# The opening of a two-layer transformer kernel: first value products from un-normed operands, in an order written out by hand

## The chip, the cores and the metric

The kernel runs on one core of one Trainium2 chip. The metric is the device time of one execution in microseconds. Lower is better. The engines are called by the names the profile uses: PE is TensorE (matrix products, 128 x 128), PEld its weight loads, DVE is VectorE, ACT is ScalarE, POOL is GpSimd, and SP is SyncE, which here issues most of the loads from memory (DMA). Each engine runs its own instructions in the order of its program, and waits on semaphores for the others. PE writes its results into eight PSUM banks of 128 x 512 f32, from which ACT or DVE has to fetch them; POOL cannot read them.

## The reference: what is computed

512 latent tokens and 256 context tokens of 1024 features go through two layers. In each layer every token is normed and modulated, goes through attention, and then through a gated feed-forward network. Only the first step of the first layer matters here:

```python
def rms_norm(x):                      # gain left out
    return x * rsqrt(mean(x * x, axis=-1) + EPS)

def modulate(x, shift, scale):
    return rms_norm(x) * (1 + scale) + shift

# layer 0: six vectors of 1024 from the conditioning, for latents (c) and for context (c_ctx)
sh_a, sc_a, g_a, sh_f, sc_f, g_f = split(silu(c) @ mod_w[0] + mod_b[0], 6)
a_lat, a_ctx = modulate(x, sh_a, sc_a), modulate(ctx, csh_a, csc_a)
p = a @ even_w_in                     # 1024 -> 1952; its last 512 columns are the values v
```

The norm factor of a token is one number for the whole token, and stands to the left of the product with the weights: `(r * x * (1 + scale) + shift) @ w` is `r * ((x * (1 + scale)) @ w) + shift @ w`.

## The kernel before

Activations lie with features on the partitions: `X[k]` is the k-th of eight tiles of 128 features by 768 tokens (columns 0 to 511 latents, `LATS`; 512 to 767 context, `CTXS`). Every f32 product is made of three products of the fast f32r kind: each operand is split into a high part (a cast) and a low part (the rest), and high x high, high x low and low x high are summed in PSUM (`three`, lines 780 to 783; `mm3`, lines 319 to 327).

The opening is lines 774 to 932. `mods_pe` (lines 180 to 204) makes the scale (component 1) and shift (component 0) vectors of layer 0. One vector comes in four chunks of 256 features, and a chunk takes four loads of 256 KB, eight products of 32 rows each (line 192), a copy out of PSUM by ACT (line 194), small products with `pick` that bring the chunk onto partitions (line 196), and two additions on DVE (line 200). `mods_pe` is a generator, and `next(scales)` or `next(shifts)` writes one chunk into the program.

The latent columns of all eight X tiles are loaded first and normed (`rms`, line 775): ACT squares each tile, DVE sums the squares, PE adds them over the partitions (line 370), ACT and DVE make the reciprocal root, PE spreads it over all partitions (line 454), and ACT copies it to `r` (line 379). Then, for each k, `scaled` (lines 789 to 795) multiplies X[k] by scale and by r on DVE, ACT casts the high part into `A[k][0]`, and DVE subtracts to get the low part `A[k][1]`. `start_products` (line 785) multiplies token tile t of A[k] by the weights of the values, `w_start[k]` (128 x 512, split on ACT and DVE by `split`), and sums over k into the bank `ov[t]`. There are six token tiles, so six of the eight banks are held for the whole opening. The other two (`PM`, lines 872 to 874) serve all that passes through. The shift reaches the values as a product `shift @ w_start` (line 915), which is copied, split, and added to each of the six banks by two more products (line 926). `put_vs` (lines 857 to 859) copies the six banks to the value tiles `VN` in 24 pieces of 128 x 128, on DVE and ACT in turn.

`A[k]` with two shift columns behind it (`shifted_columns`, lines 797 to 804) is then the operand of the first projections (`project_shifted`, lines 817 to 831, whose products are lines 325 to 327). They need all eight A[k], a free bank, and a weight tile (`load_w`: a load of 512 KB into the buffer `wr`, a cast on ACT, a subtraction on DVE). Beside the projections DVE and POOL compute further modulation vectors as dot products with `cond`, which `load_cond` (lines 162 to 164) loads and passes through Silu behind the opening.

What sets the order: instructions are written in program order, and a planner places each on its engine by a model of the time, so later instructions can move ahead on an engine while an earlier one waits. Where the code says `with in_order(...)` (lines 652 and 653) the instructions written inside it keep their written order on the engines named; others may still be placed between them. In the kernel before, nothing of the opening is written inside such a block. Buffers come in rings by tag (line 37): for example 12 of tag `st`, 3 of `wr`, 3 each of `wh` and `wl`, 8 of `p`, 24 of `b`. A load into a ring waits until an older tile of it has been read for the last time.

Of the kernel before, what the change touches and what calls it, by code (L numbers as in the profile page):

```python
# [15 lines left out]
ON_PE, ON_DVE, ON_ACT = mybir.EngineType.PE, mybir.EngineType.DVE, mybir.EngineType.Activation  # L16
P = 128
D = 1024
# [83 lines left out]
def hybrid_kernel(ctx: ExitStack, tc, I, out):  # L102
# [77 lines left out]
    def mods_pe(l, comp, get, both=None):  # L180

        one = float(comp in (1, 4))
        for v in range(2):
            MOD[l, comp, v] = T(f"mod{l}{comp}{v}", [P, 8]) if both is None else both[:, :, v]
        for c in range(4):
            o = get()
            for k in range(KT):
                if k % 2 == 0:
                    w = T("st" if l == 0 and comp < 2 else ("ph", "pl")[k // 2 % 2], [P, 512])
                    dma(w, I["mod_wp"][PE_MODS.index((l, comp)), c, k // 2])  # L190
                g = slice(32 * (k % 4), 32 * (k % 4) + 32)
                PE.matmul(o[g, :NX], cond_col[:, k], w[:, NX * (k % 2) : NX * (k % 2) + NX], start=k < 4, stop=k > 3)
            t, d = T("p", [P, NX]), get()
            S.copy(t, o[:, :NX])
            for m in range(2):
                PE.matmul(d[:, 2 * m : 2 * m + 2], t[:, m * P : (m + 1) * P], pick, start=True, stop=True)
            for v in range(2):
                r = MOD[l, comp, v][:, 2 * c : 2 * c + 2]
                at = l * 48 + comp * 8 + 2 * c
                V.scalar_tensor_tensor(r, d[:, :4].rearrange("p (m x) -> p m x", x=2)[:, :, v], one,  # L200
                                       modb[:, at : at + 2], op0=ALU.add, op1=ALU.add)
                for m in range(2):
                    MOD[l, comp, v, 2 * c + m] = r[:, m : m + 1]
            yield
# [569 lines left out]
    r = B(tag="nb")  # L774
    rms(X, LATS, r, lambda: PS("t"))
# [9 lines left out]
    def start_products(k, w, tiles):  # L785
        for t in tiles:
            three(ov[t], [x[:, t * P : (t + 1) * P] for x in A[k]], w, k == 0, k == KT - 1)

    def scaled(k, v, c):

        t = B(tag="p")
        h, lo = A[k]
        V.scalar_tensor_tensor(t[:, c], X[k][:, c], MOD[0, 1, v, k], r[:, c], op0=ALU.mult, op1=ALU.mult)
        S.copy(h[:, c], t[:, c])
        V.tensor_tensor(lo[:, c], t[:, c], f(h[:, c]), op=ALU.subtract)
# [61 lines left out]
    def put_vs(vs, kt, o):  # L857
        for p in range(4):
            copy(vs[p][:, kt * P : (kt + 1) * P], o[:, p * P : (p + 1) * P])

# [17 lines left out]
    def load_pair(c):  # L878

        h, lo = (T(x, [P, 2, 512], F32R) for x in ("wh", "wl"))  # L880
        for i in range(2):
            raw = T(("ph", "pl")[i], [P, 512])
            dma(raw, I["w_start"][2 * c + i])
            raws.append(raw)
            ws.append(split(raw, dst=(h[:, i], lo[:, i])))

    def products(c, v):

        for k in (2 * c, 2 * c + 1):
            scaled(k, v, (LATS, CTXS)[v])  # L890
            start_products(k, ws[k], ((0, 1, 2, 3), (4, 5))[v])

    scales, shifts = mods_pe(0, 1, PM), mods_pe(0, 0, PM, shift)
    next(scales)
    load_pair(0)
    next(scales)
# [34 lines left out]
    for t in range(6):  # L931
        put_vs(VN, t, ov[t])
# [1046 lines left out]
```

## Time and profile before

| what | value |
|---|---|
| median of 3 runs | 1563.28 us (1561.6 to 1563.68) |
| span of the profiled execution | 1559.6 us |
| its own time beside the span | the profile gives none beyond the span; the runs lie 2.0 to 4.1 us above it |
| instructions | 26600 |
| PE busy | 1521.7 us, 98% of the span |
| DVE, ACT, POOL busy | 1172.4 (75%), 805.4 (52%), 281.4 us (18%) |
| mean granted PE clock | 0.996 |
| first value product on PE | 23.02 us |
| first product of the first projection | 76.86 us |

The span is the time from the first to the last instruction of one profiled execution. A row of the timeline gives start, length, engine, line, operation, what is written and read, and, in brackets, the idle time before it and what ended that. "x16" means that sixteen instructions were merged into the row. Products are pipelined, so the length of one (0.39 us) is more than the distance to the next (0.23 us). An f32 product that is not split shows as two instructions.

### The profile page before, as it was taken

The numbers are of one execution on the slowest core, as the hardware profiler recorded it, in microseconds if no ns is written. First come the engines' busy times: TensorE is split into PE (matmuls) and PEld (weight loads), VectorE is DVE, ScalarE is ACT, GpSimd is POOL, SyncE is SP. The second block draws the span as 40 slices with busy tenths as digits, with TensorE's granted clock in tenths as the row PEclk, the third lists the DMA queues.
The fourth block names the chain that finished last, engine by engine and source line by source line (L and its number), as shares of the span: only waits on it lengthen the run. The fifth ranks groups of instructions, "written<-read, shape, count | busy, mean of one in ns | idle before, by whom it ended". The sixth has DMA issues, their size and how long they took to land.

```text
span 1559.6 us, 26600 instructions
## 1 busy us (share of the span) xinstructions
PE 1521.7 (98%) x9942; PEld 1355.6 (87%) x9942; DVE 1172.4 (75%) x2348; ACT 805.4 (52%) x1639; POOL 281.4 (18%) x317
## 2 busy tenths in 40 slices
PE   6999989999999999999999999999999999999998
PEld 4687867887998999998999999877789999899997
DVE  4495887576698497896878777888877778678686
ACT  5355588776474243242423345557767445454453
POOL 0173634333000010111111110381002000000000
PEclk9999999999999999999999999999999999999999
DMA  9458263104453554756666655140015223324232
GB/s 327 146 165 260 65 166 91 24 7 162 137 201 96 172 192 155 241 162 219 195 231 235 232 200 193 43 146 2 1 53 165 60 94 125 98 92 129 83 101 88
DMA packets 82129, 216.63 MB, mean 139 GB/s; under 512 B 10832, under 2 KB 18896, under 8 KB 82000
## 3 DMA queue, kind: packets, MB, share of 16 engines
q1 hardware_dynamic: 66640, 163.02, 32.8%
q0 software_dynamic: 13056, 48.77, 9.2%
q10 hardware_dynamic: 2304, 3.15, 0.5%
q8 instruction: 78, 1.28, 0.4%
q14 instruction: 51, 0.42, 0.1%
HBM read 187.10 MB, written 23.07 MB: 135 GB/s over the span
## 4 chain that ended last, share of the span: by engine, by line
PE 88%; DVE 6%; DMA 4%; issue 1%; ACT 1%; SPq 0%; DVEq 0%; ACTq 0%
PE pso L537 5%; PE pss L1416 4%; PE psd L325 4%; PE pss L325 4%; PE pss L1415 4%; PE pss L1414 4%; PE pss L326 4%; PE psd L326 4%; PE pss L327 4%; PE psd L327 4%; PE psd L1416 3%; PE psd L1415 3%; PE psd L1414 3%; PE pst L1414 3%; PE pst L1416 3%; PE pst L1415 3%
## 5 line engine op out<-in xcount | busy, mean ns | idle before, releaser
L312 ACT CAST wh<-wr 128x512 fp32r<-128x512 f32 (+2 forms) x139 | 106.0, 777 | 196.7 <-PE pss L326 37.5
L313 DVE TENSOR_TENSOR wl<-wr,wh 128x512 fp32r<-128x512 f32 (+2 forms) x136 | 126.5, 936 | 69.9 <-ACT wh L312 69.1
L543 ACT ACTIVATE p<-p,sm 128x512 f32<-128x512 f32 (+3 forms) x144 | 104.9, 729 | 29.9 <-DVE sm L547 29.2
L1415 PE MATMUL pss<-b,wh 128*128 128x384 f32 (+1 forms) x302 | 93.5, 310 | 0.0
L1414 PE MATMUL pss<-b,wh 128*128 128x384 f32 (+1 forms) x302 | 93.2, 309 | 0.0
L1416 PE MATMUL pss<-b,wl 128*128 128x384 f32 (+1 forms) x302 | 92.8, 310 | 0.1
L326 PE MATMUL psd<-b,wh 128*128 128x512 f32 (+3 forms) x253 | 86.2, 341 | 0.0
L537 PE MATMUL pso<-ph,b 128*64 128x256 f32 (+1 forms) x400 | 77.0, 351 | 1.0 <-DVE ph L475 0.8
L537 PE MATMUL pso<-pl,b 128*64 128x256 f32 (+1 forms) x400 | 77.0, 351 | 0.1
L325 PE MATMUL psd<-b,wh 128*128 128x512 f32 (+3 forms) x213 | 75.8, 357 | 0.2 <-DVE b L475 0.2
L327 PE MATMUL psd<-b,wl 128*128 128x512 f32 (+3 forms) x213 | 74.5, 351 | 0.0
L326 PE MATMUL pss<-b,wh 128*128 128x256 f32 (+3 forms) x223 | 72.8, 327 | 0.0
L769 PE MATMUL pss<-st,st 128*128 128x512 f32 (+2 forms) x264 | 68.6, 375 | 3.7 <-DVE sm L547 3.4
L325 PE MATMUL pss<-st,wh 128*128 128x512 f32 (+2 forms) x212 | 71.9, 339 | 0.0
L327 PE MATMUL pss<-st,wl 128*128 128x512 f32 (+2 forms) x212 | 71.8, 339 | 0.0
L1416 PE MATMUL psd<-b,wl 128*128 128x384 f32 (+1 forms) x226 | 70.8, 313 | 0.4 <-DVE wl L1402 0.4
L1415 PE MATMUL psd<-b,wh 128*128 128x384 f32 (+1 forms) x226 | 70.7, 313 | 0.0
L1414 PE MATMUL psd<-b,wh 128*128 128x384 f32 (+1 forms) x226 | 70.5, 312 | 0.0
L1401 ACT CAST wh<-ph 128x512 fp32r<-128x512 f32 x80 | 46.4, 620 | 40.1 <-DVE ph L1436 14.4
L1401 ACT CAST wh<-wr 128x1024 fp32r<-128x1024 f32 x40 | 42.1, 1053 | 39.2 <-PE pss L326 10.1
L1401 ACT CAST wh<-pl 128x512 fp32r<-128x512 f32 x80 | 45.9, 619 | 30.6 <-PE pst L1415 9.7
L484 PE MATMUL pst<-ident_r,p 128*128 128x128 f32 x346 | 58.0, 276 | 2.0 <-ACT p L543 0.9
(655 smaller groups left out, 5328.7 us busy)
## 6 DMA issues: line engine op xcount, KB each, us to landing
wr<-in_w_gu_dram SPq DMA_DIRECT2D x88, 512.0 KB, 4.0
wr<-in_w_out_dram SPq DMA_DIRECT2D x32, 512.0 KB, 3.5
wr<-in_w_dn_dram SPq DMA_DIRECT2D x64, 256.0 KB, 2.8
p<-home SPq DMA_DIRECT2D x40, 384.0 KB, 4.7
home<-p POOLq DMA_DIRECT2D x40, 384.0 KB, 5.1
nb<-in_mod_w_dram POOLq DMA_DIRECT2D x48, 256.0 KB, 3.8
rope<-in_mod_w_dram POOLq DMA_DIRECT2D x24, 512.0 KB, 4.3
wr<-in_w_in_dram SPq DMA_DIRECT2D x21, 512.0 KB, 4.8
```

Source lines behind the costliest of these rows:

```text
L312: S.copy(h, r)
L313: (G if eng else V).tensor_tensor(lo, r, f(h), op=ALU.subtract)
L325: PE.matmul(o, wh[:, k], mh[:, c], start=first and k == 0, stop=False)
L326: PE.matmul(o, wh[:, k], ml[:, c], start=False, stop=False)
L327: PE.matmul(o, wl[:, k], mh[:, c], start=False, stop=last and k == n - 1)
L537: ins = PE.matmul(o[64 * i : 64 * i + 64, c], v(kt), t, start=n == 0, stop=n == len(moving[i]) - 1)
L543: S.activation(p[:, c], p[:, c], AF.Exp, bias=nm, scale=-1.0, accum_out=dn)
L769: PE.matmul(o, x, k, start=i == 0, stop=i == 1)
L1401: S.copy(h, t)
L1414: PE.matmul(o, wh, xh, start=first and k == 0, stop=False, skip_group_check=not first)
L1415: PE.matmul(o, wh, xl, start=False, stop=False, skip_group_check=not first)
L1416: PE.matmul(o, wl, xh, start=False, stop=k == 3, skip_group_check=not first)
```

## The change

The opening is written anew. The main parts are these.

- The values are multiplied from un-normed operands. `unnormed(k)` casts X[k] times scale (ACT) and subtracts (DVE); `start_products` uses these, and the norm factor is applied when the banks are fetched (`put_values`), as a factor per token. The operands of the later projections are still normed: `normed_upper` and `normed_lower` make them behind the spread of the norm, the low part for odd k on POOL.
- `with in_order(ON_PE, ON_ACT, ON_DVE)` fixes the order of the opening on three engines. The modulation products stand between the value products, each chunk in two steps: up to ACT's copy, and from the `pick` products on.
- The first scale chunk is computed in two halves of 128 features, and its weights are laid out for that in memory.
- X[k] is loaded whole, in the order of use, together with w_start[k]. The first shift chunk goes into the three `wr` buffers and one of `st`.
- Products of zeros (`keep_running`) run on PE at the start, 9, 2 and 4 of them.
- The bias `shift @ w_start` is no longer added to the banks by products. Two products for each of the two rows spread it, ACT copies it into `cond`, and `put_values` adds it, on DVE for the latent tiles, on POOL for the context tiles.

```diff
     X = [B() for _ in range(KT)]
-    for k in range(KT):
-        dma(X[k][:, LATS], I["xc"][k, :, LATS])
     modb = const("modb", [P, 96])
-    ident_r = const("ident", [P, P], F32R)
+    ident_r = T("ident_r", [P, P], F32R)
...
+    def mod_weights(l, comp, c, tags=None):
+        ws = []
+        tags = tags or (("st",) * 4 if l == 0 and comp < 2 else ("ph", "pl") * 2)
+        for k in range(0, KT, 2):
+            ws.append(T(tags[k // 2], [P, 512]))
+            dma(ws[-1], I["mod_wp"][PE_MODS.index((l, comp)), c, k // 2])
+        return ws
...
+            ws = fetched.get(c) or mod_weights(l, comp, c)
+            single = (l, comp, c) == (0, 1, 0)
+            for part in range(2 if single else 1):
+                n = 1 if single else 2
+                o = get()
+                for k in range(KT):
+                    w = ws[2 * part + k // 4][:, P * (k % 4) :] if single else ws[k // 2][:, NX * (k % 2) :]
+                    g = slice(32 * (k % 4), 32 * (k % 4) + 32)
+                    PE.matmul(o[g, : n * P], cond_col[:, k], w[:, : n * P], start=k < 4, stop=k > 3)
+                t = T("p", [P, NX])
+                S.copy(t[:, : n * P], o[:, : n * P])
+                if halves:
+                    yield
+                d = get()
...
-    r = B(tag="nb")
-    rms(X, LATS, r, lambda: PS("t"))
+    r, rcol = B(tag="nb"), T("rcol", [P, NT // P])
...
+    def start_products(k, tiles):
+        for t in tiles:
+            three(ov[t], [x[:, t * P : (t + 1) * P] for x in U[k]], ws[k], k == 0, k == KT - 1)
+    def unnormed(k):
+        h, lo = U[k] = A[k] if k < 6 else [B(F32R, "p") for _ in range(2)]
+        for v, c in enumerate((LATS, CTXS)):
+            S.activation(h[:, c], X[k][:, c], AF.Copy, scale=MOD[0, 1, v, k])
+            V.scalar_tensor_tensor(lo[:, c], X[k][:, c], MOD[0, 1, v, k], f(h[:, c]), op0=ALU.mult, op1=ALU.subtract)
+    def normed_upper(k):
+        t = normed[k] = B(tag="p")
+        for v, c in enumerate((LATS, CTXS)):
+            V.scalar_tensor_tensor(t[:, c], X[k][:, c], MOD[0, 1, v, k], r[:, c], op0=ALU.mult, op1=ALU.mult)
+        S.copy(A[k][0][:, :NT], t)
+    def normed_lower(k):
+        (G if k % 2 else V).tensor_tensor(A[k][1][:, :NT], normed[k], f(A[k][0][:, :NT]), op=ALU.subtract)
...
+    def start_norm():
+        d = PM()
+        for i in range(NT // P):
+            PE.matmul(d[:, i : i + 1], sums[0][:, i * P : (i + 1) * P], ones[:, :1], start=True, stop=True)
+        S.activation(rcol, d[:, : NT // P], AF.Sqrt, bias=eps, scale=1.0 / D)
+        V.reciprocal(rcol, rcol)
+    def start_spread():
+        for i in range(0, NT // P, 4):
+            n = min(4, NT // P - i)
+            d = PM()
+            spread(d, [rcol[:, x : x + 1].to_broadcast([P, P]) for x in range(i, i + n)])
+            S.copy(r[:, i * P : (i + n) * P], d[:, : n * P])
+    def start_bias():
+        bias = PM()
+        for k in range(KT):
+            PE.matmul(bias[32 * (k % 4) : 32 * (k % 4) + 32], shift[:, k], raws[k], start=k < 4, stop=k > 3)
+        raw = cond[:, :, :NX]
+        S.copy(raw, bias.rearrange("p (v c) -> p v c", v=2))
+        part = [T(x, [P, 512], F32R) for x in ("wh", "wl")]
+        hi, lo = (x.rearrange("p (v c) -> p v c", v=2) for x in part)
+        S.copy(hi, raw)
+        V.tensor_tensor(lo, raw, f(hi), op=ALU.subtract)
+        return part
+    def spread_bias(part):
+        for v in range(2):
+            o = PM()
+            for i, x in enumerate(part):
+                PE.matmul(o, pick_r[:, v : v + 1].to_broadcast([P, P]), x, start=i == 0, stop=i == 1)
+            S.copy(cond[:, v, 512:], o)
+    def put_values(tiles):
+        for t in tiles:
+            for p in range(4):
+                c, at = slice(p * P, (p + 1) * P), slice(t * P, (t + 1) * P)
+                row = cond[:, t // 4, 512 + p * P : 640 + p * P]
+                if t < 4:
+                    V.scalar_tensor_tensor(VN[p][:, at], ov[t][:, c], rcol[:, t : t + 1], row, op0=ALU.mult, op1=ALU.add)
+                else:
+                    S.activation(VN[p][:, at], ov[t][:, c], AF.Copy, scale=rcol[:, t : t + 1])
+                    G.tensor_tensor(VN[p][:, at], VN[p][:, at], row, op=ALU.add)
...
+    early = fetched_w[1, 0] = [T("st", [P, 512]) for _ in range(4)]
+    for m in range(2):
+        for i in (2 * m, 2 * m + 1):
+            dma(early[i], I["mod_wp"][0, 0, i])
+        fetch_x(m)
+    ident_raw = cond[:, 0, :P]
+    dma(ident_raw, I["ident"])
+    for c, ks in ((1, (2, 3)), (2, (4, 5)), (3, (6, 7))):
+        fetched_w[1, c] = mod_weights(0, 1, c)
+        for k in ks:
+            fetch_x(k)
+    fetched_w[0, 0] = mod_weights(0, 0, 0, ("wr", "wr", "wr", "st"))
...
+    def keep_running(n):
+        for _ in range(n):
+            PE.matmul(ov[0], idle[:, :P], idle, start=True, stop=True)
+    with in_order(ON_PE, ON_ACT, ON_DVE):
+        keep_running(9)
+        next(scales)
+        keep_running(2)
+        next(scales)
+        split_start(0)
+        unnormed(0)
+        keep_running(4)
+        start_products(0, (0, 1))
+        next(scales)
+        start_products(0, (2,))
+        next(scales)
+        split_start(1)
+        unnormed(1)
...
+        split_start(7)
+        start_products(4, (3, 4, 5))
+        start_products(5, (0, 1))
+        next(shifts)
+        start_products(5, (2,))
+        next(shifts)
+        unnormed(7)
+        start_products(5, (3, 4, 5))
+        start_norm()
+        shifted_columns(0)
+        start_products(6, (0, 1))
+        next(shifts)
+        start_products(6, (2,))
+        next(shifts)
+        start_spread()
+        start_products(6, (3, 4, 5))
+        shifted_columns(1)
+        normed_upper(0)
+        normed_upper(1)
+        normed_lower(0)
+        normed_upper(2)
+        normed_lower(1)
+        start_products(7, (0, 1))
+        next(shifts)
+        start_products(7, (2,))
+        next(shifts)
+        shifted_columns(2)
+        normed_upper(3)
+        normed_lower(2)
+        normed_upper(4)
+        normed_lower(3)
+        start_products(7, (3, 4))
+        next(shifts)
+        start_products(7, (5,))
+        next(shifts)
+        shifted_columns(3)
+        normed_upper(5)
+        normed_lower(4)
+        part = start_bias()
+        normed_upper(6)
+        normed_lower(5)
+        normed_upper(7)
+        normed_lower(6)
+        normed_lower(7)
+        spread_bias(part)
+    VN = [B() for _ in range(4)]
+    put_values((0, 1, 4, 2, 3, 5))
     for v in range(2):
         load_cond(v)
-    VN = [B() for _ in range(4)]
     sets = [(new_q(), new_k()) for _ in range(2)]
-    for t in range(6):
-        put_vs(VN, t, ov[t])
```

More of the change, by code (lines that the diff above doesn't have):

```diff
@@ L185, in mods_pe @@
         for c in range(4):
[L186 to L203, printed above, removed]
@@ L876, in hybrid_kernel @@
     raws, ws = [], []
[L878 to L893, printed above, removed]
@@ L916, in hybrid_kernel, with fetch @@
[L916 to L926 removed]
+    def fetch(c):
+        for i, k in enumerate((2 * c, 2 * c + 1)):
+            dma(X[k], I["xc"][k])
+            raws.append(T(("ph", "pl")[i], [P, 512]))
+            dma(raws[-1], I["w_start"][k])
@@ new lines, in spread_bias @@
+    def spread_bias(part):
+        for v in range(2):
+            o = PM()
[12 more added lines that the diff above has]
+                    G.tensor_tensor(VN[p][:, at], VN[p][:, at], row, op=ALU.add)
```

117 lines of the change are left out of this document (71 added, 46 removed).

## The prediction

> **What bounds the kernel now.** I read the span first, then busy time by stage (after each engine's busy time the count; then granted clock, DMA share, GB/s), then the chain of waits of the opening, then its instructions in order of time.
>
> ```profile
> span 1559.6 us, 26600 instructions
> ...
> core 0: us, PE busy (x) PEld busy (x) DVE busy (x) ACT busy (x) POOL busy (x), PEclk, DMA share, GB/s
> 0.00:23.00 23.00, 8.29 (x52) 5.08 (x52) 9.42 (x20) 12.86 (x22) 1.93 (x9) 1.00 0.92 300
> 23.00:77.00 54.00, 52.40 (x300) 37.06 (x301) 24.86 (x62) 18.57 (x42) 5.14 (x24) 0.97 0.60 208
> 80.00:1550.00 1470.00, 1455.96 (x9556) 1309.11 (x9556) 1131.25 (x2249) 770.95 (x1568) 274.31 (x284) 1.00 0.42 134
> ```
>
> PE is the bound: from 80 to 1550 us it lacks 14 us of 1470. Only the opening has room: 14.7 us idle in the first 23, with the loads at 92%. So what the opening gains in the moment at which PE begins the first projection reaches the end nearly whole, and what it loses does too. That moment is 76.86 us (the L325 row further down). The chain of waits of the opening (start, length, what):
>
> ```profile
> 2.61 5.08 DMA b<-in_xc_dram
> ...
> 13.10 1.88 PE pst L370 x8
> ...
> 16.65 3.56 PE pst L192 x28
> ...
> 23.02 0.51 PE pss L781
> ```
>
> The first value product (L781) stands behind the latent norm: loads of X, squares and seven sums on ACT and DVE, column sums on PE (L370), and only then the modulation products (L192). From here on PE is nearly full, but not at speed:
>
> ```profile
> 24.36 0.63 PE L781 MATMUL pss<-wh,b 128*128 128x512 f32 x1
> 24.79 0.63 PE L782 MATMUL pss<-wl,b 128*128 128x512 f32 x1
> ...
> 38.50 0.39 PE L781 MATMUL pst<-wh,b 128*128 128x512 f32 x1
> 38.73 0.40 PE L782 MATMUL pst<-wl,b 128*128 128x512 f32 x1
> ...
> 24.00:25.00 1.00, 1.00 (x4) 0.81 (x3) 0.35 (x1) 0.00 (x0) 0.00 (x0) 0.50 0.78 217
> ```
>
> Start to start is 0.43 us at a granted clock of 0.50 and 0.23 us later. The opening therefore has 144 products (8 k, 6 token tiles, 3 each) worth 144 x 0.233 = 33.6 us at full clock.
>
> **The change, part by part.**
>
> *The first product.* Un-normed operands need only one half of the first scale chunk, X[0] and w_start[0]. Ahead of that half lie cond_col, pick, modb and two 256 KB loads, 0.7 MB. Before, the second X tile was 0.66 MB deep in the queue, the third 0.92 MB.
>
> ```profile
> 4.51 1.29 ACT L357 ACTIVATE p<-b 128x512 f32<-128x512 f32 x2 [1.17 <-DMA b<-in_xc_dram]
> 66.02 1.07 PE L192 MATMUL pst<-st,cond_col 128*32 128x256 f32 x16
> 67.21 0.37 ACT L194 COPY p<-pst 128x256 f32<-128x256 f32 x1 [11.52 <-PE pst L192]
> 67.64 0.61 PE L196 MATMUL pso<-pick,p 128*128 128x2 f32 x4 [0.55 <-ACT p L194]
> 68.28 0.23 DVE L200 SCALAR_TENSOR_TENSOR nb<-pso,modb 128x2 f32<-128x2 f32 x2 [8.20 <-PE pso L196]
> ```
>
> Two tiles were there by 5.15, the third at 7.69; I take 6.7 for the half chunk. Then half of 1.07 on PE, about 0.4 to copy on ACT, 0.4 for the pick, 0.23 on DVE: scale at 8.4. ACT then casts w_start[0] and the high half of X[0], 0.62 each (the L794 row below): first product at about 9.8 instead of 23.02. Bounds 8.3 and 11, from the two landings. The zero products (15 x 0.43 = 6.4 us at most) lie in waits: nine of them end near 5.3, before the weights; if the weights came at 4.5 they would cost 0.8.
>
> *PE from there.* 33.6 for the products; 7.5 modulation chunks x 1.07 = 8.0; their picks about 0.45 each (under the row's 0.61, which holds a wait), 3.6. The norm's sums and spread are as follows, for 2 and 2 columns; six of each make about 2.5.
>
> ```profile
> 45.91 0.50 PE L370 MATMUL pst<-ones,p 128*128 128x1 f32 x4
> ...
> 47.77 0.43 PE L454 MATMUL pso<-ident_r,sm 128*128 128x128 f32 x2
> ```
>
> Sum 47.7, so 57.5 if nothing waits. The loads keep ahead: X, w_start and all four scale chunks are 9.7 MB, at the 300 GB/s of the first 23 us about 32 us with a lag of one or two, and PE reaches k = 6 only at about 43. SP issues eight loads fewer (X whole in place of halves), in the order of use. DVE has 8 x 1.14 (un-normed low halves, as the L793 rows below), 7 x 0.95 (square sums) and 8 x 0.69 (w_start's low halves, as L921 below), 21.3 us in the 39 up to the norm; ACT has no more.
>
> *What waits, and who is behind it.* PE, ACT and DVE now keep the written order. After the spread (about 49) every k costs DVE one scaling and, for even k, one subtraction, and ACT one cast, all of 768 columns.
>
> ```profile
> 29.77 1.41 DVE L793 SCALAR_TENSOR_TENSOR p<-b,mod,nb 128x512 f32<-128x512 f32 x2
> ...
> 59.21 0.87 DVE L793 SCALAR_TENSOR_TENSOR p<-b,mod,nb 128x256 f32<-128x256 f32 x2
> ...
> L794 ACT CAST b<-p 128x512 fp32r<-128x512 f32 x8 | 4.8, 618 | 3.1 <-DVE p L793 3.1
> L315 ACT ACTIVATE wh<-wr 128x1024 fp32r<-128x1024 f32 x2 | 2.1, 1058 | 0.3 <-PE psd L926 0.3
> ...
> L1113 POOL TENSOR_TENSOR st<-b,st x16: 1809/1837/1853, 237.0 to 345.5; 64x768 fp32r<-64x768 f32 x16
> ```
>
> DVE: 1.41/2 + 0.87/2 = 1.14, and about 0.95 for a subtraction; ACT between 0.62 and 1.06, so 0.85; POOL, for odd k, takes 1.84 a piece (the row has 64 partitions), twice DVE's time, and has 2.3 for each before one is late. Eight scalings and four subtractions are 12.9 us of DVE, against some 14 us of PE work (products of k = 6 to 7, two shift chunks). That would be cover, but the engines stand in line. The copy of shift chunk 2 on ACT is queued behind the cast for k = 2, which waits for DVE; PE's pick behind it waits about 1.2 us; chunk 3 behind k = 4 likewise about 1.8; with smaller waits 3.5. Products done near 61.
>
> *The tail.*
>
> ```profile
> 68.24 1.84 PE pst L915 x12
> ...
> 72.26 0.59 ACT L917 COPY cond<-pst 128x512 f32<-128x512 f32 x1 [4.07 <-PE pst L915]
> 72.88 0.62 ACT L920 CAST wh<-cond 128x512 fp32r<-128x512 f32 x1
> 73.53 0.69 DVE L921 TENSOR_TENSOR wl<-cond,wh 128x512 fp32r<-128x512 f32 x1 [4.36 <-ACT wh L920]
> 74.08 0.85 PE L926 MATMUL pss<-wh,pick_r 128*128 128x512 f32 x3
> ...
> 76.86 0.28 PE L325 MATMUL pst<-b,wh 128*128 128x258 f32 x1
> ```
>
> Before, twelve bias products (74.08 to 76.86) filled PE up to the projection. Now: bias sums end near 63.1; ACT copy and cast, 64.6; DVE low half, 65.3; then on DVE the scalings for k = 6 and 7, 67.6; ACT cast for k = 7, 68.5; and only behind it, on ACT, the copy of the first bias row, 0.59: 69.1. All eight PSUM banks are held until this copy (six by the values, one and one by the rows), so the first projection starts at 69.1: 7.8 us earlier than 76.86. From 63.1 to 69.1 PE does four products of 0.23 us.
>
> *Half clock behind the tail.*
>
> ```profile
> 1045.77 0.50 PE L769 MATMUL pss<-st,st 128*128 128x512 f32 x1 [2.24 <-DVE sm L547]
> ...
> 1047.00:1048.00 1.00, 1.00 (x9) 0.75 (x7) 1.00 (x5) 0.88 (x3) 1.00 (x2) 0.83 1.04 391
> 1048.00:1049.00 1.00, 1.00 (x4) 0.81 (x4) 0.97 (x4) 1.00 (x4) 1.00 (x2) 0.50 0.96 336
> ...
> 1051.00:1052.00 1.00, 0.91 (x5) 0.35 (x3) 1.00 (x5) 0.59 (x1) 0.92 (x2) 0.96 1.04 399
> ```
>
> After an idle time of 2.24 us the clock was halved for some 3.4 us, which loses 1.7. A tail of 6 us with 0.93 at work and a last idle time near 3 us I price the same: 7.8 - 1.7 = 6.1.
>
> The Trainium skill (TensorE: Matmul & The Clock Gate, "What's actually happening") says that the clock falls only after an idle window of about 3.4 us, free-running. By that rule the tail might keep its clock and the gain would be 7.8; the trace's gap of 2.24 us speaks against needing so long a gap.
>
> *Covered parts.* Evacuation: 24 pieces as before, 16 on DVE at 0.2 to 0.4 (512 columns cost 0.70), 8 on ACT, 8 additions on POOL (of 128 columns, so well under the 1.84 of 768); they run beside the projection, which needs its second bank only some 3 us in. Uncovered, the 16 would cost 3 to 6 us. The three w_in tiles, loaded at 32.5 before, now wait until the first shift chunk leaves wr, near 39:
>
> ```profile
> 32.51 1.38 SPq L135 DMA_DIRECT2D wr<-in_w_in_dram  x3
> ...
> wr<-in_w_in_dram SPq DMA_DIRECT2D x7, 512.0 KB, 6.5
> ...
> L316 DVE SCALAR_TENSOR_TENSOR wl<-wr,wh 128x1024 fp32r<-128x1024 f32 x2 | 2.4, 1219 | 0.3 <-ACT wh L315 0.3
> ...
> 74.25 0.80 SPq L135 DMA_DIRECT2D cond<-in_cond_dram  x2
> ```
>
> They land near 46, and are wanted near 69: covered by 20 us. Their DVE part (1.22 each) falls into the full DVE chain, 0 to 1.4 us, of which I take none or 0.1. SP's load of cond, behind the last POOL addition now, leaves near 75 as before (74.25), so the modulation dot products that need it come 6 to 8 us later against PE; DVE has gaps for them, priced at nothing, else up to 2 us.
>
> Sum: 7.8 - 1.7 - 0.1 = 6.0; span 1559.6 - 6.0 = 1553.6. The median of the runs, 1563.28, lies 3.7 above the span; the profiled execution shows no time beyond it, and I keep that difference: **1557.3 us**. The tail of the trace after 1550 is not touched.
>
> **The rivals.**
>
> *The clock holds across the tail.* For it: four products break the idle time up, and only its last piece is near 3 us. Against it: 2.24 us at 1045.77 were enough. 1563.3 - 7.8 = 1555.5. Chance 0.17. The Trainium skill's rule (TensorE: Matmul & The Clock Gate, "What's actually happening") would give this time too.
>
> *The tail closes up.* If ACT and DVE keep pace, only the product sum counts: 57.5 plus bias sums 1.9, ACT and DVE 1.9, four products 0.9, a copy 0.6, makes 62.8, a start 14 us earlier, 12.3 after the 1.7 for the clock: 1551. For it: 12.9 us of DVE under 14 us of PE. Against it: the written order on three engines. Chance 0.17.
>
> *It comes to nothing that can be told.* First products still at half clock, since between the ninth zero product and the first real one PE is more idle than busy (loses 1.7), and two weight casts inside the DVE chain (2.4): 6.0 - 4.1 = 1.9, 1561.4. Or the zero products don't wake the clock at all, which is the same 1.7. Chance 0.15.
>
> *Slower: a weight cast put in ahead of its load.* The casts for the projection aren't in the written order; where they go between its instructions is planned. If one stands early on ACT, it waits there for w_in, whose load is behind the first shift chunk (39) and the queued shift chunks behind it, say at 50; ACT, then DVE and PE stand with it. From a wait of 9.1 us (6.0 + 3.1) on the kernel is slower; with 11 us lost it takes 1568. For it: wr now lands 7 to 11 us later. Against it: before, the loads were issued at 32.5 and the first product that needs them ran at 76.86. Chance 0.09.
>
> **How the numbers follow.** A difference below 0.2% (3.1 us) cannot be told from none here. Forecast 0.42, clock 0.17, closed tail 0.17: faster 0.76. Same 0.15, slower 0.09. The range leaves out half of the slower rival and a closed tail without clock loss: 1550 to 1563. The forecast's own range is 1553.5 to 1560.
>
> **What would show it.** Right: first L781-like product at 8.3 to 11 us at 0.23 us cadence, projection at 67 to 71, DVE full from 49 to 68, PE idle about 5 of the 6 us before the projection, granted clock 0.50 after it. Wrong: products at 0.43 us after 10; a load ending a PE wait after 12 us; ACT or DVE waiting for wr inside the ordered stretch; PE idle after 80 us much above 14.

## The result, and the profile after

The changed kernel takes **1574.86 us** (median of 4 runs, 1573.19 to 1579.61) against 1562.44 us before (4 runs, 1561.11 to 1563.68). The ratio is 1.0085, with a 95% interval of 1.0068 to 1.0101: slower, where I had predicted 1557.3 us and a range that ends at 1563. The profiled execution is the slowest of the four (1579.61 us, span 1577.7), so its trace shows some 5 us more than the median does.

Busy time by stage of the changed kernel, columns as before:

```profile
core 0: us, PE busy (x) PEld busy (x) DVE busy (x) ACT busy (x) POOL busy (x), PEclk, DMA share, GB/s
0.00:23.00 23.00, 19.83 (x112) 13.60 (x113) 8.47 (x21) 10.94 (x22) 1.60 (x9) 1.00 0.90 323
23.00:78.00 55.00, 42.73 (x263) 28.18 (x262) 30.89 (x56) 26.72 (x45) 13.90 (x28) 0.92 0.55 194
80.00:1568.00 1488.00, 1468.38 (x9571) 1314.82 (x9570) 1132.84 (x2260) 770.97 (x1567) 279.54 (x293) 1.00 0.40 132
```

The first 23 us are as forecast: PE is busy for 19.83 us instead of 8.29. Then PE idles for 12.3 of 55 us, where before it idled for 1.6 of 54, and part of its work is at half clock. The instructions of PE in order of time (start, length, engine, line, operation, idle time before and what ended it):

```profile
1.64 4.21 PE L996 MATMUL pss<-p 128*128 128x512 f32 x9 [1.64 <-DVE p L991]
...
10.62 0.50 PE L793 MATMUL pss<-wh,b 128*128 128x512 f32 x1 [1.48 <-ACT b L807]
...
11.74 0.39 PE L793 MATMUL pss<-wh,b 128*128 128x512 f32 x1
11.97 0.40 PE L794 MATMUL pss<-wl,b 128*128 128x512 f32 x1
...
35.97 0.79 PE L793 MATMUL pss<-wh,b 128*128 128x512 f32 x1 [3.79 <-ACT b L807]
...
63.48 0.61 PE L208 MATMUL pst<-pick,p 128*128 128x2 f32 x4 [1.87 <-ACT p L203]
...
68.52 0.61 PE L208 MATMUL pst<-pick,p 128*128 128x2 f32 x4 [1.04 <-ACT p L203]
...
78.00 0.55 PE L338 MATMUL pst<-b,wh 128*128 128x258 f32 x1 [2.95 <-ACT cond L950]
...
125.80 0.39 PE L340 MATMUL pst<-b,wl 128*128 128x258 f32 x1 [2.88 <-DVE wl L326]
```

The first value product runs at 10.62, and the cadence, the distance from start to start, is 0.23 us soon after (11.74 to 11.97). But the first projection starts at 78.00, 1.1 us later than before instead of 7.8 earlier. Two rows need an explanation, the wait of 3.79 at 35.97 and that of 2.88 at 125.80. DVE, in order of time:

```profile
23.72 0.95 DVE L373 TENSOR_TENSOR p<-p,p 128x768 f32<-128x768 f32 x1
33.45 0.17 DVE L1897 TENSOR_SCALAR sink_neg<-sink_bc 128x16 f32<-128x16 f32 x1 [8.79 <-DMA sink_bc<-in_sink_bc_dram]
...
92.27 0.49 DVE L740 SCALAR_TENSOR_TENSOR st<-pst,sm,st 64x256 fp32r<-64x256 f32 x1 [6.76 <-ACT st L450]
```

The same two instructions in the kernel before, where the load left at 33.93 and DVE didn't wait:

```profile
43.18 0.17 DVE L1732 TENSOR_SCALAR sink_neg<-sink_bc 128x16 f32<-128x16 f32 x1
...
33.93 0.43 SPq L135 DMA_DIRECT2D sink_bc<-in_sink_bc_dram  x1
```

And the loads that SP issues in the changed kernel:

```profile
28.28 0.33 SPq L135 DMA_DIRECT2D sink_bc<-in_sink_bc_dram  x1
...
85.49 0.80 SPq L135 DMA_DIRECT2D cond<-in_cond_dram  x2
```

**First accident.** `sink_neg` is an instruction of the second layer, 16 numbers per partition, 0.17 us. The planner placed it on DVE between two square sums of the opening. Its small load is issued only at 28.28, behind 256 KB loads, and lands at 33.4. DVE stands for 8.79 us, all that is written behind it stands too, and PE runs dry for 3.79 us. Behind that gap the clock was 0.50 (granted, 36 to 41.5 us), which loses 2.9 us more.

**Second accident.** The loads of cond leave at 85.49 instead of 74.25. The bias rows lie in the tile of `cond`, so its load waits for the last evacuation. ACT, in which Silu follows, and DVE, whose dot products need it, stand: DVE idles 6.76 us up to 92.27 and then is behind. At 125.80 PE waits for a low half of a weight that DVE makes, and behind this wait the clock was 0.50 to 0.75 (127 to 131 us), 1.7 us lost. POOL shows why the evacuation ends so late:

```profile
71.69 1.81 POOL L821 TENSOR_TENSOR b<-p,b 128x768 fp32r<-128x768 f32 x1
77.45 4.68 POOL L821 TENSOR_TENSOR b<-p,b 128x768 fp32r<-128x768 f32 x1 [3.96 <-ACT b L817]
82.08 3.38 POOL L961 TENSOR_TENSOR b<-b,cond 128x128 f32<-128x128 f32 x8
```

The table below follows PE through the traces (start of the first instruction of each kind, us; the last two columns are the first and the last product of `mm3` that reads a weight's high half and a tile `st` and writes a bank `pss`; the last one lies near the end of the second layer). The stage is the time from the first projection to the first score product. PE does 720 to 722 products in it in every kernel.

| kernel | median of runs | first projection | first scores | stage | first such product | last |
|---|---|---|---|---|---|---|
| before | 1562.44 | 76.9 | 190.8 | 113.9 | 385.8 | 1532.1 |
| after | 1574.86 | 78.0 | 202.5 | 124.5 | 399.6 | 1549.7 |
| e1_sink | 1570.01 | 73.6 | 197.1 | 123.5 | 392.8 | 1541.9 |
| e2_cond | 1572.35 | 78.9 | 196.3 | 117.4 | 393.9 | 1543.1 |
| e3_sink_cond | 1562.93 | 73.8 | 188.4 | 114.6 | 384.8 | 1532.9 |
| e4_awake | 1567.92 | 75.8 | 193.9 | 118.1 | 390.0 | 1538.3 |
| e5_rows | 1562.38 | 75.4 | 194.9 | 119.5 | 391.1 | 1540.3 |
| e6_early | 1567.74 | 73.4 | 195.8 | 122.4 | 391.9 | 1539.9 |
| e7_nozero | 1560.79 | 75.5 | 189.5 | 114.0 | 385.4 | 1533.0 |
| e8_weights | 1563.65 | 72.3 | 191.0 | 118.7 | 386.9 | 1534.2 |
| e9_early_weights | 1562.41 | 70.5 | 187.9 | 117.4 | 384.4 | 1535.9 |

So in the trace 1.1 us are lost by 78 us and 10.6 more by the first scores. Of these 10.6, 3.4 are more idle time of PE (4.4 us against 1.1) and 5.8 are half clock (none before). The other 6 us come later, in stages whose code the change leaves as it is. The profiled execution is 4.8 us above the median of its kernel, and the one of before 0.8 below. But in the traces of all ten other kernels the stretch from the first scores to the last mark is 1.9 to 6.7 us longer than in that of before (1341.3 us). What costs this time isn't shown.

Beside the experiments the kernel before took 1562.73, 1562.11 and 1562.36 us (medians of 17, 29 and 23 runs). A difference of two kernels that didn't run side by side is therefore uncertain by some 0.6 us more than their spread says.

### The profile page after: what moved, and what is told of

Same layout as the page of the kernel before. It is cut to its first block, busy times and chain, and to the rows that moved or that the text cites. A ratio compares the mean times of both kernels' runs of the same rounds, so it can differ in the third digit from the quotient of the medians.

```text
span 1577.7 us, 26652 instructions
## 1 busy us (share of the span) xinstructions
PE 1535.2 (97%) x9965; PEld 1360.3 (86%) x9965; DVE 1178.1 (75%) x2347; ACT 811.2 (51%) x1641; POOL 297.0 (19%) x329
## 4 chain that ended last, share of the span: by engine, by line
PE 76%; DVE 9%; DMA 6%; issue 2%; ACT 1%; POOL 0%; DVEq 0%; ACTq 0%; SPq 0%; POOLq 0%
PE pso L550 4%; PE pss L1581 4%; PE pss L1579 4%; PE pss L1580 4%; PE psd L338 4%; PE psd L339 4%; PE psd L340 4%; PE pss L338 3%; PE pss L339 3%; PE pss L340 3%; PE psd L1581 3%; PE psd L1580 3%; PE psd L1579 3%; PE pst L1581 3%; PE pst L1579 3%; PE pst L1580 3%
## 5 line engine op out<-in xcount | busy, mean ns | idle before, releaser
L325 ACT CAST wh<-wr 128x512 fp32r<-128x512 f32 (+2 forms) x139 | 105.9, 776 | 197.1 <-PE pss L339 49.5
L550 PE MATMUL pso<-ph,b 128*64 128x256 f32 (+1 forms) x400 | 76.9, 351 | 1.1 <-DVE ph L488 0.8
L339 PE MATMUL pss<-b,wh 128*128 128x256 f32 (+3 forms) x223 | 73.4, 329 | 0.0
L1566 ACT CAST wh<-wr 128x1024 fp32r<-128x1024 f32 x40 | 42.0, 1050 | 38.3 <-PE pss L339 10.2
```

Source lines behind the costliest of these rows:

```text
L325: S.copy(h, r)
L339: PE.matmul(o, wh[:, k], ml[:, c], start=False, stop=False)
L550: ins = PE.matmul(o[64 * i : 64 * i + 64, c], v(kt), t, start=n == 0, stop=n == len(moving[i]) - 1)
L1566: S.copy(h, t)
```

## The experiments

**e1_sink: the small load first.**

```diff
     modb = const("modb", [P, 96])
+    sink_bc = const("sink_bc", [P, 16])
 ...
-    sink_bc = const("sink_bc", [P, 16])
     sink_neg = ...
```

> Edit: the load of sink_bc (8 KB) is written at the start, ahead of the first loads, so that the small DVE instruction on it (sink_neg, L1897), which the planner put into the opening, has nothing to wait for. Theory (a planned-in instruction blocks the ordered engines): DVE's wait of 8.79 us at 24.66 us goes, and with it PE's wait of 3.79 us at 32.2 and the half clock behind it (36 to 41.7 us, 2.85 lost), so the first projection starts 6.6 us earlier than in the changed kernel, near 71.4 us, and the time is about 1574.9 - 6.6 = 1568.3. Rival (the end of the opening is bound by its own chain on DVE and ACT in any case): first projection near 78, time near 1575.

Measured: 1570.01 us (1569.76 to 1571.03, 5 runs), ratio to before 1.0049 (1.0037 to 1.0062), 4.85 us below the changed kernel. DVE in this kernel:

```profile
3.95 0.18 DVE L1897 TENSOR_SCALAR sink_neg<-sink_bc 128x16 f32<-128x16 f32 x1 [2.36 <-DMA sink_bc<-in_sink_bc_dram]
...
87.54 0.49 DVE L741 SCALAR_TENSOR_TENSOR st<-pst,sm,st 64x256 fp32r<-64x256 f32 x1 [5.83 <-ACT st L451]
```

Nothing waits near 35 any more, and the first projection starts at 73.57, 4.4 us earlier. The wait for cond is still there; its load leaves at 80.69. PE has a gap for the second pick, as in the changed kernel:

```profile
58.43 0.61 PE L209 MATMUL pst<-pick,p 128*128 128x2 f32 x4 [1.87 <-ACT p L204]
```

and behind it, by stretches, half clock for part of the next five us:

```profile
60.00:65.00 5.00, 5.00 (x35) 2.62 (x37) 2.92 (x7) 2.67 (x5) 4.50 (x8) 0.73 0.00 0
```

The changed kernel had a clock of 1.00 behind the same gap. So half clock takes back 1.7 us here. It takes another 1.7 at the first value products: they follow each other at 0.43 us with a clock of 0.50 (12 to 14 us), although the same zero products run ahead of them. The first accident is shown. It is worth 4.85 us against 6.6 expected.

**e2_cond: bias rows in tiles of their own, so that cond loads in the opening.**

```diff
-        raw = cond[:, :, :NX]
+        raw = T("p", [P, 2, NX])
 ...
-            S.copy(cond[:, v, 512:], o)
+            rows.append(T("st", [P, 512]))
+            S.copy(rows[v], o)
 ...
         spread_bias(part)
+        for v in range(2):
+            load_cond(v)
```

> Edit: the bias and its rows are kept in tiles of their own, so that cond can be loaded during the opening, and its Silu is written last in the ordered block; the blocked DVE instruction of the opening is left as it is. Theory (late cond): Silu ends near 81 instead of 93.3, DVE's idle time of 6.76 us at 85.5 goes, and so do PE's wait of 2.88 us for a weight's low part at 125.8 and the half clock behind it (1.7): about 1574.9 - 4.6 = 1570.3, with the first projection unchanged near 78. Rival (what is lost in the projection stage comes from the planner's other order there, not from cond): PE still waits near 125, time near 1575.

Measured: 1572.35 us (1571.59 to 1572.8), ratio 1.0062 (1.0050 to 1.0075), 2.5 us below the changed kernel. The stage shrinks from 124.5 to 117.4 us and the wait near 125 is gone; one of 1.0 us for a low half is left, at 116.16. The opening got worse: one of the two loads of cond now leaves ahead of the small one (26.41), which leaves at 30.25 instead of 28.28:

```profile
37.22 0.79 PE L793 MATMUL pss<-wh,b 128*128 128x512 f32 x1 [5.26 <-ACT b L807]
```

This wait is 1.5 us longer than the 3.79 of the changed kernel, so 2.5 us is probably too low a price for the second accident.

**e3_sink_cond: both.**

> Edit: both of the above. If both causes are separate, their gains add: 1574.9 - 6.6 - 4.6 = 1563.7, close to the kernel before (1562.4), first projection near 71.4, and from there to the first attention product about 117 us (113.9 before, 124.5 in the changed kernel). Rival (one of the two hides the other, or the planner's order costs by itself): above 1567.

Measured: 1562.93 us (1560.86 to 1565.8, 12 runs), ratio 1.0002 (0.9990 to 1.0015). That is as before, and 11.9 us below the changed kernel; the two alone give 4.85 and 2.5. Part of the 4.6 us between 11.9 and their sum is seen in the traces: the 1.5 us more of wait in e2, and 3.4 us at half clock ahead of the projection in e1 (11 to 15 and 59 to 63 us) where e3 has a clock of 1.00. That the half clock of e1 recurs in its other executions isn't shown. What remains of the forecast gain is the question of the next runs. PE in this kernel:

```profile
35.71 1.30 PE L202 MATMUL pst<-st,cond_col 128*32 128x256 f32 x8 [1.79 <-DMA st<-in_mod_wp_dram]
...
59.28 0.61 PE L209 MATMUL pst<-pick,p 128*128 128x2 f32 x4 [1.88 <-ACT p L204]
...
69.91 0.49 PE L952 MATMUL pst<-wl,pick_r 128*128 128x512 f32 x1 [1.11 <-DVE wl L942]
...
73.81 0.55 PE L339 MATMUL pst<-b,wh 128*128 128x258 f32 x1 [2.95 <-ACT st L954]
```

The first projection starts at 73.81, 4.7 us later than my 69.1. ACT, in the tail:

```profile
67.03 0.58 ACT L938 COPY p<-pso 128x512 f32<-128x512 f32 x1
67.64 0.62 ACT L941 CAST wh<-p 128x512 fp32r<-128x512 f32 x1
68.16 1.05 ACT L329 ACTIVATE wh<-wr 128x1024 fp32r<-128x1024 f32 x1
69.12 1.03 ACT L326 CAST wh<-wr 128x1024 fp32r<-128x1024 f32 x1
70.68 1.06 ACT L329 ACTIVATE wh<-wr 128x1024 fp32r<-128x1024 f32 x1 [0.53 <-PE pso L952]
71.64 1.55 ACT L818 CAST b<-p 128x768 fp32r<-128x768 f32 x2
73.09 0.57 ACT L954 COPY st<-pst 128x512 f32<-128x512 f32 x1
```

Three planned weight casts, 3.1 us, stand between the cast of the bias and the row copy that frees the bank. DVE in the same time:

```profile
68.29 1.57 DVE L942 TENSOR_TENSOR wl<-p,wh 128x512 fp32r<-128x512 f32 x1 [1.17 <-ACT wh L941]
69.78 2.19 DVE L817 SCALAR_TENSOR_TENSOR p<-b,mod,nb 128x512 f32<-128x512 f32 x4
...
75.30 0.95 DVE L822 TENSOR_TENSOR b<-p,b 128x768 fp32r<-128x768 f32 x1
76.17 3.18 DVE L962 SCALAR_TENSOR_TENSOR b<-pss,rcol,st 128x128 f32<-128x128 f32 x12
```

ACT's casts of k = 6 and 7 (71.64) need the scalings on DVE, which end at 71.97, and these stand behind the low half of the bias. That took 1.57 us instead of the 0.69 of before (the L921 row of the prediction). So the weight casts lie mostly in time in which ACT would have waited for DVE. The clock in two stretches:

```profile
70.00:75.00 5.00, 2.05 (x8) 1.61 (x9) 5.00 (x7) 4.45 (x7) 1.74 (x1) 0.74 0.73 252
75.00:80.00 5.00, 5.00 (x28) 5.00 (x27) 5.00 (x17) 4.62 (x11) 5.00 (x7) 0.58 0.81 302
```

0.26 of 2.05 and 0.42 of 5.00 make 2.6 us lost (the 3.5 in the expectation of e6 is too high).

**e4_awake: e3 with 24 zero products in the tail's gaps** (a zero operand, added into a finished bank: the values stay as they are).

```diff
+    def stay_awake(n):
+        for _ in range(n):
+            PE.matmul(ov[5][:96], none, ws[7][0], start=False, stop=True, skip_group_check=True)
```

> Edit: as the kernel with both repairs, and 24 products with a stationary operand of zeros (96 columns) are added to a finished bank in the three idle times of PE at the end of the opening, which changes no value. Theory (the clock falls in these idle times): granted clock 1.00 from the first projection on, instead of 0.50 for 4.7 us, 2.35 us gained against the kernel with both repairs, about 1561.3. Rival (the first projection waits for DVE's weight parts anyway, or zeros don't keep the clock): no difference, about 1563.7.

Measured: 1567.92 us (1567.26 to 1570.38), ratio 1.0038 (1.0025 to 1.0051): slower than e3, against both expectations. The granted clock in two stretches, and then in the one where PE lost time:

```profile
59.00:66.00 7.00, 6.82 (x29) 4.33 (x30) 3.21 (x7) 2.44 (x5) 4.77 (x7) 0.51 0.01 4
66.00:76.00 10.00, 9.76 (x50) 5.52 (x50) 8.18 (x13) 6.24 (x9) 4.73 (x8) 1.00 0.65 209
...
120.00:140.00 20.00, 17.33 (x125) 12.27 (x124) 9.20 (x20) 13.95 (x30) 3.57 (x7) 1.00 0.98 298
```

The zero products do keep the clock at 1.00 through the tail. But here the clock had fallen before it, behind the wait of 1.84 us for the pick at 59.18. The same wait of 1.88 in e3 (59.28, shown there) was followed by a clock of 1.00. And PE, late by 2.0 us, idled 2.67 us at 120 to 140, where the loads are at 98%: waits of 1.1, 0.9 and 0.6 us for modulation weights. Why the later start meets them isn't shown. A lower clock in this one execution can't explain the median: the mean granted clock was 0.994 to 0.996 over the five runs of e4, and 0.991 to 0.996 over the twelve of e3.

**e5_rows: e3 with `spread_bias` ahead of the scalings of k = 6 and 7.**

> e3_sink_cond with one block moved: the four bias row products and their two copies stand ahead of the scalings and casts of k = 6 and 7 on PE, ACT and DVE instead of behind them. Theory (the end of the tail is a matter of the written order: the first projection waits for the row copy, which stands on ACT behind the casts of k = 6 and 7): the row copies end near 71.2 instead of 73.7, the first projection starts there, 2.5 us earlier, and k = 6 and 7 are ready about when it reaches them: 1560.4. Rival (DVE and POOL set the end, not the order): the projection starts earlier but stands at k = 6 or 7 until about the same moment, 1563.

Measured: 1562.38 us (1561.0 to 1569.64, 12 runs), ratio 1.0001 (0.9989 to 1.0013). The rival's time. The trace is of the slowest of twelve executions, so I don't read the start at 75.4 as typical. In it the tail is shorter, as the theory had it: from the first row product to the first projection it takes 2.9 us (72.49 to 75.36) instead of 5.5 in e3 (68.31 to 73.81). But a scale chunk comes 2.24 us late (36.52), and the half clock behind that loses 3.4 us. Why the other executions gain nothing isn't shown.

**e6_early: e3 with norm, spread and shift chunks earlier.**

```diff
+        start_norm()
         next(shifts)
         start_products(5, (2,))
         next(shifts)
+        start_spread()
         unnormed(7)
 ...
         part = start_bias()
+        normed_upper(5)
+        normed_lower(4)
+        spread_bias(part)
```

> e3_sink_cond with the second half of the opening rewritten: the norm's column sums, root and spread stand ahead of the products of k = 5 (2 to 5) instead of inside those of k = 6, shift chunks 1 to 3 lie inside the products of k = 6 and 7 with their copies ahead of the casts on ACT, and the bias rows stand ahead of k = 6 and 7. Theory (what is left of the forecast gain is lost in the tail, since the DVE chain of 13 us starts only at 52.4 behind the spread, and the half clock of 3.5 us follows from the tail's gaps): the spread ends near 48.5, DVE is through near 63, the first projection starts at 65 to 67 instead of 73.8 and no half clock follows: 1552 to 1556. Rival (the half clock stays, and stops at k = 6 and 7 give half of it back): 1559. Rival (the stage behind the opening is bound by loads or by the planner's order, and takes it all back): 1563.

Measured: 1567.74 us (1565.17 to 1571.93, 12 runs), ratio 1.0038 (1.0024 to 1.0052). The first projection still starts at 73.4, and the long waits of PE ahead of it and behind it (from 72 to 197 us: what for, in total, times, longest) are

```profile
PE pss L341 <- DVE wl L327: 2.9, 1, 2.9
PE pst L341 <- DVE wl L330: 2.8, 1, 2.8
PE pst L339 <- ACT st L954: 2.5, 1, 2.5
```

The theory falls. Ahead of the tail nothing was won: the copy of the raw bias starts at 67.93, 0.9 us later than in e3. A scale chunk came 2.11 us late (36.72), and the half clock behind that lost 3.4 us. In the tail the planner put three weight casts ahead of the row copies on ACT, and DVE, at 9.8 to 10 of every 10 us from 70 to 120, was late with the low halves.

**e7_nozero: e3 without the fifteen zero products.**

> e3_sink_cond without the fifteen zero products. Theory (they wake the clock and cost nothing, as they lie in waits for loads): the first modulation and value products run at half clock for a while, some 2 to 3.5 us of them, so 1 to 1.7 us are lost: 1564.3. Rival (the opening is bound by loads and by ACT and DVE there, so PE's speed in its first microseconds doesn't matter): 1563.

Measured: 1560.79 us (1558.76 to 1562.21, 12 runs), ratio 0.9985 (0.9971 to 0.9998), the best of all. PE in the beginning:

```profile
10.41 0.79 PE L794 MATMUL pss<-wh,b 128*128 128x512 f32 x1 [2.52 <-ACT b L808]
11.00 0.63 PE L795 MATMUL pss<-wl,b 128*128 128x512 f32 x1
11.43 0.63 PE L796 MATMUL pss<-wh,b 128*128 128x512 f32 x1
```

Without them the first six products do run at 0.43 us and end 1.0 us later. Yet this costs nothing: e3 waits 1.79 us for a scale chunk at 35.7, and e7 has no wait for a load there and is at the second pick at 59.12, e3 at 59.28. That e7 starts the projection 1.7 us later (75.5) is the clock again: behind a wait of 1.87 us for this pick it was 0.50 up to 66 us, 3.4 us lost, where e3 had 1.00. Whether e7 is really faster than e3 (they ran in different comparisons, and their intervals overlap) stays open.

**e8_weights: e7 with e5's order, the first weights split by hand, and the evacuation in order.**

```diff
         start_products(7, (2,))
+        first_weights(0)
 ...
         part = start_bias()
+        spread_bias(part)
         normed_upper(6)
 ...
         normed_lower(7)
+        put_values((0, 1, 4, 2, 3, 5))
+        first_weights(4)
```

> e7_nozero with the first two weight tiles of the projection split by hand (the first inside the products of k = 7, the second behind the subtractions), the bias rows ahead of k = 6 and 7 as in e5_rows, and the evacuation written in order behind the subtractions. Theory (the planned weight casts, 3.1 us on ACT and 3.6 us on DVE in the tail, hold the row copy and the first products up): row copies end near 71, the first projection starts there instead of 75.5, and its stage keeps the 114 us that it takes in e7_nozero: 1556.5. Rival (VectorE is full from 70 to 120 in all of these kernels and sets the pace of that stage, so an earlier start only makes PE wait there for low halves of weights): start near 71 to 72, stage 117 to 118 us, 1560.5.

Measured: 1563.65 us (1561.06 to 1567.77, 12 runs), ratio 1.0008 (0.9998 to 1.0018). The first projection starts at 72.3, 3.2 us earlier than in e7, and its stage takes 118.7 us instead of 114.0. The 3.2 us aren't all owed to the edit: e8 has a clock of 1.00 behind its wait of 1.88 us for the second pick, where e7 lost 3.4 us. Against e3, which lost none there either, it starts 1.5 us earlier. The rival had 117 to 118 us, for another reason than the trace shows: there is no wait for low halves. A stretch of PE:

```profile
120.00:140.00 20.00, 17.68 (x113) 11.40 (x112) 8.45 (x19) 12.83 (x28) 3.13 (x7) 1.00 0.99 318
```

PE idles 2.32 us between 120 and 140, where before it idled none, with the loads at 99%: 1.4 us for a copy of a modulation chunk, 0.9 us for modulation weights. In the whole stage PE idles 2.3 us more than in e7 and loses 0.9 less at half clock (1.2 against 2.1). So some 3.3 us of the longer stage lie in time where the profile shows PE as busy at full clock, and stay open.

**e9_early_weights: e6 with the same three steps, without zero products.**

> e6_early without zero products and with the same three steps as e8_weights. Theory: the two waits of 2.8 and 2.9 us for low halves of weights in e6_early go, the first projection starts at 70 to 71: 1557 to 1560. Rival (VectorE sets the pace): the waits move to later weights, stage 120 us or more, 1564 to 1567.

Measured: 1562.41 us (1560.32 to 1565.53, 12 runs), ratio 0.9999 (0.9989 to 1.0010), 5.3 us below e6. The two waits for low halves are gone, and the first projection starts at 70.46. From there the gain melts: 6.4 us against before at the first projection, 2.9 at the first scores, 1.4 at the next mark of the table, and at the last one this execution is 3.8 us behind. Of the 3.5 us lost by the first scores, 1.6 are half clock (70.5 to 73.5) and 0.6 more idle time; the other 1.3 stay open. The last part is seen in the feed-forward networks and the second layer, whose code no kernel here changes. The first wait below isn't there in before; the clock is that behind a gap near 1048 us:

```profile
660.51 0.59 PE L1587 MATMUL psd<-b,wl 128*128 128x384 f32 x1 [2.23 <-DVE wl L1573]
```

```profile
1055.00:1056.00 1.00, 1.00 (x5) 0.81 (x4) 0.84 (x2) 0.07 (x1) 0.58 (x1) 0.50 0.01 2
```

## Why the prediction was wrong

*First product, 9.8 (8.3 to 11), cadence 0.23.* Right: 10.62 and 0.23. That the zero products lie in waits is right too. That they make the cadence sure is not: with the same fifteen ahead, the first products ran at 0.43 us in e1 and e4. That half clock there would cost 1.7 us was wrong: e7 lost 1.0 us at the first products and got it back by the second pick.

*"DVE has 21.3 us in the 39 up to the norm."* **This is the first step that failed.** The sum holds only what is written in the block. I wrote myself that the casts for the projection "aren't in the written order" and that "where they go between its instructions is planned", and made it a rival with a chance of 0.09. That rival had the mechanism right and its place wrong: not a weight cast on ACT, but an instruction of the second layer on DVE. e1 prices it at 4.85 us alone. I had not looked in the trace of before for such an instruction, although `sink_neg` stood at 43.18 there, in the middle of the opening.

*"SP's load of cond ... leaves near 75 as before ... priced at nothing, else up to 2 us."* **The second step that failed.** It left at 85.49. My own tail had the row copies at 69, the additions of POOL behind them, and POOL still with the last subtraction; I took each addition for short, and not that they begin behind a subtraction that takes 4.68 us (77.45) and not 1.84. Without the first accident the load would still have left late, at 80.69 (e1). With that accident out of the way the step costs 7.1 us (e1 to e3), alone 2.5 (e2), not 0 to 2.

*"The loads keep ahead."* Nearly: in e3 one scale chunk is 1.79 us late at 35.7, and the same chunk 2.24 us in e5 and 2.11 in e6.

*What waits, 3.5 us.* Nearly right: 2.9 us, on the chunks named, but 1.87 for chunk 2 and 1.04 for chunk 3 where I had 1.2 and 1.8.

*The tail, 6.0 us from the bias sums to the projection.* It took 6.8 in e3 (67.03, the copy of the raw bias, to 73.81), mainly since the low half of the bias took 1.57 us and not 0.69. This 0.8 is one part of the 4.7 us by which 69.1 was too early. The first product (10.38) is 0.6 late. Between it and the copy of the raw bias PE idles 5.06 us, 1.6 more than the 3.5, owing to the late chunk. And it is busy for 51.59 us there, 1.8 more than the sum gives (47.7, and 2.1 for the bias sums).

*Half clock behind the tail, 1.7 us.* Right in kind, too small: it was 2.6 us in e3. The Trainium skill (TensorE: Matmul & The Clock Gate, "What's actually happening") has the clock fall only after an idle window of about 3.4 us, free-running. Here gaps of 1.84 us (e4) and 1.87 us (e1) were enough, and one of 1.88 us (e3) was not. That the window runs free agrees with this, that it must be idle for 3.4 us does not, and the rival in which the clock holds across the tail failed in e3.

*"What the opening gains reaches the end nearly whole."* **The third step, which failed in part.** I read it from one row: PE lacked 14 of 1470 us, so PE is the bound. But DVE in before was at 39.30 of 40 us between 80 and 120, and the loads at 1.01 from 120 to 140:

```profile
80.00:120.00 40.00, 39.49 (x215) 34.13 (x216) 39.30 (x73) 21.64 (x52) 28.76 (x24) 1.00 0.54 162
120.00:140.00 20.00, 20.00 (x145) 15.64 (x145) 8.75 (x17) 12.29 (x24) 4.09 (x8) 1.00 1.01 307
```

PE just keeps pace with both there. A projection that starts earlier finds the same DVE and the same loads. Of 1.4 us (e7) 1.3 arrive at the scores, of 3.1 us (e3) 2.4, of 6.4 us (e9) 2.9, of 4.6 us (e8) nothing. Part of what is lost is known: 1.6 us of half clock in e9 and 1.2 in e8, and 2.3 us of waits for modulation chunks between 120 and 140 in e8. That DVE and the loads take the rest is argued, not shown: no run makes one of them lighter. And behind the scores all these traces lose 1.9 to 6.7 us against before, in code that is the same.

Without the accidents, the change comes to nothing that can be told (e3). I had that as a rival with 0.15, but for other causes (first products at half clock, weight casts in DVE's chain). e3 misses the forecast by 5.6 us. At the first scores its trace is 2.4 us ahead of before, where the forecast has 6.1 (7.8 less 1.7). The start of the projection is 4.7 us too late and the clock takes 0.9 us more, and the stage gives some of this back. The 2.4 us don't last to the end (ratio 1.0002), and where they go is open.

## What to carry to other kernels

In a stretch with a written order, list what the planner put between the instructions on each engine, and for each of these when its load is issued: one instruction of 0.17 us with a late load cost 4.85 us here, where the whole change was forecast to gain 6.0. Move every load of a constant that is needed anywhere up, and give scratch data a tile that no later load waits for. Before counting an earlier start as gain, look at the stage behind it: if a second engine or the loads are full there, the gain may be spent where PE catches up with them, as with the waits of e8.

## What the runs showed of the hardware that I had not expected

The clock's fall doesn't follow from the length of a gap alone. Behind the same gap near 1046 us (2.24 us in before, 2.14 in e3, 2.13 in e9) before lost 1.7 us, e3 nothing, and e9 3.2 us, its clock at 0.50 from 1050 to past 1055. Behind a wait of 1.84 to 1.89 us for the pick of a shift chunk e1, e2 and e5 lost 1.7 us, e4 and e7 3.4, and the changed kernel, e3 and e8 nothing. This alone can move the time of one execution by 0.2%.

A subtraction of 128 x 768 f32 on POOL took 1.80 to 1.85 us where DVE was idle for part of it. It took 4.68 us while DVE worked through subtractions and low halves without a break, instructions that read two tiles (77.45; the same 4.68 at 73.26 in e3). In e3 it ended 1.77 us after DVE had gone over to fetching banks (76.17), as if it had begun only then. The same distance is 1.77 us in the changed kernel, 1.78 in e1, 1.76 in e2, 1.79 in e4 and 1.80 in e8. It works the other way round too: in e3 and in e8 the low half of the bias on DVE, 0.69 us alone (e6, 69.19), ended 0.55 us after the end of a subtraction that POOL had under way (67.50 and 68.52). A full DVE doesn't always hold POOL up so long: between scalings (59.74 in the changed kernel) the subtraction took 2.27 us. What decides this isn't shown.

The granted clock of the profile doesn't show every slow start: in e7 the first products follow each other at 0.43 us, the cadence that goes with 0.50 in before, while the clock column has 1.00 for these microseconds.
